# One level of Strassen's algorithm in the gate and up blocks of a gated network, with the way down in three parts

## The chip, the core and the metric

The kernel runs on one core of one Trainium2 chip. The metric is device time in microseconds (us) of one execution. Before the change it is 920.8 us, the median of three runs (919.7 to 921.03). One more execution was recorded by the hardware profiler; it took 920.15 us, and its trace spans 918.4 us from the first to the last instruction. All rows below come from that one execution.

## The reference

One layer of a streaming encoder on 512 tokens of width 1024, all in float32: a mixer (sliding-window attention beside gated linear attention), cross attention on 256 memory tokens, and a gated network with 2816 hidden units, each added to the residual, then a last normalisation. The change concerns the gated network and what stands at its two ends:

```python
def _rms(t, w):
    y = t * lax.rsqrt(jnp.mean(t * t, axis=-1, keepdims=True) + EPS)
    return y * w

def _swiglu(h, w_gate, w_up, w_down):
    return (jax.nn.silu(h @ w_gate) * (h @ w_up)) @ w_down

x = x + _swiglu(_rms(x, norm_ffn_w), w_ffn_gate, w_ffn_up, w_ffn_down)   # 1024 -> 2816 -> 1024
return _rms(x, norm_final_w)
```

## The kernel before, in words

Activations lie transposed: eight tiles of 128 features by 512 tokens are the residual (`res`). A float32 product is made of three products in a rounded format (`F32R`): each operand is split into a rounded high part and the rest (`split`, lines 93 to 100: a ScalarE copy, then a VectorE subtraction), and high x high, high x low and low x high are added up in PSUM. A block of 128 outputs by 512 tokens with a contraction over 1024 is thus 8 x 3 = 24 matmuls of 512 columns (`block`).

Weights come in units of 128 x 1024 float32 (512 KB). `unit` takes three tiles from the pool `wp`, loads R by SyncE's DMA queue, and splits it into H and L. Each of the tags R, H, L has three slots; a slot is free when the last instruction that uses its tile is done. PSUM has four banks with the tag `mm`, two `s`, one `t`, one `o`.

The program is traced in order, and a planner then makes a fixed order for each engine: of the instructions that are ready in its own reckoning it takes the one that stands earliest in the program, and it gives a tile any slot of its tag that is free. Where `manual_schedule` names an engine, that engine keeps the order of the program.

The stages around the change. The end of the cross attention adds to `res` (line 996) and splits `res` times the norm's weight (`weighted`, lines 97 and 98) into `zh` and `zl`. Then the gate and up blocks (lines 1007 to 1022): for each of 22 groups j of 128 hidden units, 24 matmuls for the gate and 24 for the up block, on tokens not yet divided by their root mean square. That factor comes from the norm `n2`, whose squares (ScalarE, line 195) and sums (VectorE, line 201) are written behind the blocks of j = 0; `finish` sums over partitions on TensorE, makes the root on VectorE, spreads it by TensorE, and ScalarE copies it to `n2.b` (line 224, tile `rb_n`). With `n2.b` VectorE scales the gate (line 1018), ScalarE applies Silu, VectorE multiplies by the up block (line 1020) and again by `n2.b` (line 1021), and the result is split into `ah[j]`, `al[j]`.

Last the way down: for each of eight blocks of 128 outputs, 66 matmuls over all 22 groups, the sum into `res` (line 1036), and the square for the last norm `n3`. The last block goes in two halves of 256 tokens, each with its own end of the norm, its own scaling (lines 1048 to 1054) and output DMAs.

Of the kernel before, what the change touches and what calls it, by code (L numbers as in the profile page):

```python
# [20 lines left out]
P = 128  # L21
S = 512
# [5 lines left out]
NF = DFF // P  # L28
EPS = 1e-6
NEG = -1.0e30  # L30
TGW = 328
DENSE = (10, 5, 11, 3, 1)


def build(tc, a, out):
# [56 lines left out]
    def split(hi, lo, src, scale=None):  # L92
# [3 lines left out]
        else:  # L96
# [2 lines left out]
                out=lo, in0=src, scalar=scale, in1=f(hi), op0=ALU.mult, op1=ALU.subtract  # L99
            )  # L100

    def unit_tiles():
        return [
            wp.tile([P, 1024], dt, tag=tag, bufs=3, name=uniq(tag)) for tag, dt in (("R", F32), ("H", F32R), ("L", F32R))
        ]

    def unit(src):
# [893 lines left out]
    mep_ctx.__exit__(None, None, None)  # L1001


    fp_ctx = pool("fp")
    fp = fp_ctx.__enter__()
    ah = [fp.tile([P, S], F32R, name=f"ah{j}") for j in range(NF)]
    al_ = [fp.tile([P, S], F32R, name=f"al{j}") for j in range(NF)]
    for j in range(NF):
        pg = ps_mm()
        block(pg, [(unit(a["w_fg"][j]), KC)], zh, zl)  # L1010
        pu = ps_mm()
        block(pu, [(unit(a["w_fu"][j]), KC)], zh, zl)
        if j == 0:
            for i in range(KC):
                n2.add(res[i])
            n2.finish()
        t = t2k()
        nc.vector.tensor_tensor(out=t, in0=pg, in1=n2.b, op=ALU.mult)  # L1018
        table_act(t, t, AF.Silu)
        nc.vector.tensor_tensor(out=t, in0=t, in1=pu, op=ALU.mult)  # L1020
        nc.vector.tensor_tensor(out=t, in0=t, in1=n2.b, op=ALU.mult)
        split(ah[j], al_[j], t)

    n3 = Norm("n3", S)
    for j in range(KC):
        units = []
        for k0 in range(0, NF, KC):
            nk_ = min(KC, NF - k0)
            units.append((unit(a["w_fd"][j][:, k0 * P : (k0 + nk_) * P]), nk_))

        W = S if j < KC - 1 else S // 2
        for c0 in range(0, S, W):
            cs = slice(c0, c0 + W)
            pb = ps_mm()
            block(pb[:, :W], units, [x[:, cs] for x in ah], [x[:, cs] for x in al_])
            nc.vector.tensor_tensor(out=res[j][:, cs], in0=res[j][:, cs], in1=pb[:, :W], op=ALU.add)
            n3.add(res[j][:, cs], cols=cs, last=j == KC - 1)
            if j < KC - 1:
                nc.scalar.activation(res[j], res[j], AF.Copy, scale=wo_w[:, j : j + 1])
                continue  # L1040
            n3.finish(cols=cs)
            for i in (7, 6, 0, 1, 2, 3, 4, 5):
                if i % 2 == (1 if i > 5 else 0):
                    fin = xwp.tile([P, S], F32R, tag="xw", bufs=16, name=uniq("fin"))
                    f3 = f(fin).rearrange("p (e c) -> p e c", e=2)
                o = f3[:, i % 2]
                if i == j:
                    nc.vector.scalar_tensor_tensor(
                        out=o, in0=res[i][:, cs], scalar=wo_w[:, i : i + 1], in1=n3.ps, op0=ALU.mult, op1=ALU.mult
                    )  # L1050
                elif i in (3, 5):
                    nc.gpsimd.tensor_tensor(out=o, in0=res[i][:, cs], in1=n3.b, op=ALU.mult)
                else:
                    nc.vector.tensor_tensor(out=o, in0=res[i][:, cs], in1=n3.ps, op=ALU.mult)
                if i % 2 == (0 if i > 5 else 1):
                    nc.sync.dma_start(out[i // 2][:, :, cs], f3)
    fp_ctx.__exit__(None, None, None)
    ctx.close()

# [70 lines left out]
```

## Time and profile before

| | |
|---|---|
| median of three runs | 920.8 us (919.7 to 921.03) |
| profiled execution | 920.15 us |
| its span | 918.4 us |
| TensorE matmul busy | 902.0 us (98%), 4318 matmuls |
| TensorE weight load busy | 746.2 us (81%) |
| VectorE busy | 557.3 us (61%) |
| ScalarE busy | 426.5 us (46%) |
| mean granted TensorE clock | 0.996 |
| HBM | 83.27 MB read, 93 GB/s over the span |

Matmuls are pipelined: one reports 0.39 us while the next starts 0.23 us after it. So the pace of TensorE is read from the distance of two starts, not from the duration of one, and the same holds for VectorE, where an instruction reports up to 0.09 us more than the distance to the next.

### The profile page before, as it was taken

What the parts mean: (1) busy time and instruction counts of PE and PEld (TensorE: products, weight loads), DVE (VectorE), ACT (ScalarE), POOL (GpSimd) and SP (SyncE); (2) the same over time, 40 slices, a digit from 0 to 9 for tenths busy, and PEclk for the clock granted to TensorE, in tenths of its full rate; (3) what the DMA queues carried; (4) which work ended last, traced back from release to release, by engine and by line L of the source; (5) the groups of instructions that cost most, each with busy time, mean ns of one, the idle gap of its engine ahead of it and who ended that gap; (6) DMA issues with size and microseconds to landing.
All of it is one profiled execution on the core that took longest, in us unless ns stands there. A gap on an engine that the chain in (4) does not pass through costs nothing.

```text
span 918.4 us, 11423 instructions
## 1 busy us (share of the span) xinstructions
PE 902.0 (98%) x4318; PEld 746.2 (81%) x4318; DVE 557.3 (61%) x1104; ACT 426.5 (46%) x760; POOL 7.0 (1%) x29
## 2 busy tenths in 40 slices
PE   9999999999999999999999999999999999999995
PEld 7898888887888787778888778888888888888885
DVE  6777888787343959966676996444444444323323
ACT  7576674556333838463345864222332233222220
POOL 1000000000000000000000000000000000000001
PEclk9999999999999999999999999999999999999998
DMA  7232222222222031425332223233222332333312
GB/s 249 92 115 70 69 70 69 70 69 69 92 94 91 23 115 46 144 87 155 120 115 92 70 77 107 92 97 110 92 92 92 99 107 86 99 91 103 87 41 92
DMA packets 29415, 86.11 MB, mean 94 GB/s; under 512 B 4048, under 2 KB 7760, under 8 KB 29360
## 3 DMA queue, kind: packets, MB, share of 16 engines
q1 hardware_dynamic: 29216, 85.37, 29.3%
q8 instruction: 34, 0.56, 0.3%
q14 instruction: 21, 0.17, 0.1%
q10 hardware_dynamic: 144, 0.00, 0.0%
HBM read 83.27 MB, written 2.10 MB: 93 GB/s over the span
## 4 chain that ended last, share of the span: by engine, by line
PE 89%; DVE 6%; ACT 3%; DMA 1%; issue 1%; SPq 0%; DVEq 0%; ACTq 0%
PE mm L76 80%; PE s L76 3%; PE o L76 3%; PE t L76 1%; DMA x<-in_xT 1%; DVE L L95 1%; PE t L540 1%; ACT pm L90 1%; PE mm L540 1%; DVE sl L95 1%; DVE on L743 1%; ACT H L94 0%; PE t L754 0%; DVE st L701 0%; DVE on L722 0%
## 5 line engine op out<-in xcount | busy, mean ns | idle before, releaser
L94 ACT CAST H<-R 128x1024 fp32r<-128x1024 f32 (+2 forms) x155 | 156.8, 1013 | 326.1 <-PE mm L76 251.4
L95 DVE TENSOR_TENSOR L<-R,H 128x1024 fp32r<-128x1024 f32 (+2 forms) x155 | 181.7, 1174 | 93.5 <-ACT H L94 93.1
L76 PE MATMUL mm<-xh,L 128*128 128x512 f32 x592 | 232.4, 393 | 0.0
L76 PE MATMUL mm<-xl,H 128*128 128x512 f32 x592 | 232.2, 392 | 0.0
L76 PE MATMUL mm<-xh,H 128*128 128x512 f32 x592 | 230.8, 390 | 0.0
L76 PEld LDWEIGHTS mm<-xh,H 128*128 128x128 f32 x592 | 111.2, 188 | 22.7
L76 PEld LDWEIGHTS mm<-xl,H 128*128 128x128 f32 x592 | 111.2, 188 | 22.3
L76 PEld LDWEIGHTS mm<-xh,L 128*128 128x128 f32 x592 | 111.2, 188 | 21.6
L76 PE MATMUL mm<-ah,H 128*128 128x512 f32 (+1 forms) x198 | 72.5, 366 | 0.0
L76 PE MATMUL mm<-ah,L 128*128 128x512 f32 (+1 forms) x198 | 72.4, 366 | 0.0
L76 PE MATMUL mm<-al,H 128*128 128x512 f32 (+1 forms) x198 | 72.3, 365 | 0.0
L76 PE MATMUL mm<-H,xh 128*128 128x512 f32 (+1 forms) x192 | 70.4, 367 | 0.0
L76 PE MATMUL mm<-L,xh 128*128 128x512 f32 (+1 forms) x192 | 70.3, 366 | 0.0
L76 PE MATMUL mm<-H,xl 128*128 128x512 f32 (+1 forms) x192 | 70.1, 365 | 0.0
L1020 DVE TENSOR_TENSOR t2k<-t2k,mm 128x512 f32<-128x512 f32 x22 | 15.0, 688 | 68.3 <-PE mm L76 67.6
L90 ACT ACTIVATE p<-sm,nm,sc 128x256 f32<-128x256 f32 (+1 forms) x64 | 36.3, 569 | 25.3 <-DVE es L514 20.4
L1018 DVE TENSOR_TENSOR t2k<-mm,rb_n 128x512 f32<-128x512 f32 x22 | 15.1, 691 | 44.9 <-PE mm L76 43.0
L76 PEld LDWEIGHTS mm<-ah,H 128*128 128x128 f32 x198 | 37.3, 189 | 6.1
L76 PEld LDWEIGHTS mm<-ah,L 128*128 128x128 f32 x198 | 37.3, 189 | 6.1
L76 PEld LDWEIGHTS mm<-al,H 128*128 128x128 f32 x198 | 37.3, 189 | 5.9
L76 PEld LDWEIGHTS mm<-H,xh 128*128 128x128 f32 x192 | 36.4, 190 | 5.2 <-issue 0.2
L76 PEld LDWEIGHTS mm<-L,xh 128*128 128x128 f32 x192 | 36.1, 188 | 5.3 <-DVE L L95 0.4
(299 smaller groups left out, 1365.2 us busy)
## 6 DMA issues: line engine op xcount, KB each, us to landing
R<-in_w_fg SPq DMA_DIRECT2D x22, 512.0 KB, 3.3
R<-in_w_fu SPq DMA_DIRECT2D x22, 512.0 KB, 3.3
R<-in_w_gate SPq DMA_DIRECT2D x16, 512.0 KB, 3.4
R<-in_w_fd SPq DMA_DIRECT2D x16, 512.0 KB, 3.5
x<-in_xT SPq DMA_DIRECT2D x16, 256.0 KB, 3.3
R<-in_w_q SPq DMA_DIRECT2D x8, 512.0 KB, 3.6
R<-in_w_attn_o SPq DMA_DIRECT2D x8, 512.0 KB, 3.3
R<-in_w_vg SPq DMA_DIRECT2D x8, 512.0 KB, 3.3
```

The costliest lines, as they stand in the source:

```text
L76: nc.tensor.matmul(o, lhsT=lhsT, rhs=rhs, start=start, stop=stop)
L90: last_table[0] = nc.scalar.activation(*args, **kw)
L94: nc.scalar.copy(out=hi, in_=src)
L95: nc.vector.tensor_tensor(out=lo, in0=src, in1=f(hi), op=ALU.subtract)
L540: nc.tensor.transpose(out=pt[:, i * P : (i + 1) * P], in_=prs[i // 2][:, i % 2, b * P : (b + 1) * P], identity=ident)
L743: nc.vector.scalar_tensor_tensor(out=on[t][:, vs], in0=on[t][:, vs], scalar=r[:, h : h + 1], in1=glaw, op0=ALU.mult, op1=ALU.mult)
L1018: nc.vector.tensor_tensor(out=t, in0=pg, in1=n2.b, op=ALU.mult)
L1020: nc.vector.tensor_tensor(out=t, in0=t, in1=pu, op=ALU.mult)
```

## The change

The gate and up blocks of groups 2 to 21 are made by one level of Strassen's algorithm (in Winograd's form): the two weight matrices of a group, each in two halves of the contraction, are one 2 x 2 of blocks, and the tokens, in two halves of 512 features and two halves of 256 tokens, the other. Seven products take the place of eight. Each product is 4 x 3 = 12 matmuls of 256 columns, so a group has 84 of them in place of 48 of 512. Groups 0 and 1 (`NPLAIN = 2`) stay as they were.

The token operands are sums of normalised tokens, so they need `n2.b`: `token_side` makes them once, behind the end of `n2` and ahead of the gating of group 0. `weight_side` makes the weight operands of each group: two loads, four pairs of H and L. `group` has three steps, each ended by a `yield`: products r11 and r21; then t2, t1, t3; then t4, r22 and the gating. TensorE keeps the written order: for groups 2 to 7 the first step of group j+1 stands ahead of the last step of group j; from group 8 a block of the way down stands between the second and the last step. The way down is in parts of 8, 8 and 6 groups: the first two are added to `res` between the groups, the third takes the place of the loop at the end. The pool `fw` takes the place of `wp` with three slots for R, four for H, four for L, and two of tag S for sums.

```diff
+NPLAIN = 2
-    wp = ctx.enter_context(pool("wp"))
+    wp_ctx = pool("wp", side="right")
+    wp = wp_ctx.__enter__()
...
+    wp_ctx.__exit__(None, None, None)
     fp = fp_ctx.__enter__()
+    fw_ctx = pool("fw", side="right")
+    units_from[:] = fw, (3, 4, 4)
+    PARTS = ((0, 8), (8, 16), (16, NF))
+    t0, t1 = slice(0, HS), slice(HS, S)
...
+    def token_side():
+        zn = []
+        for i in range(4):
+            t = f(fp.tile([P, 2, S], F32R, tag="a", bufs=8, name=uniq("zn")))
+            for e in range(2):
+                nc.vector.scalar_tensor_tensor(
+                    out=t[:, e], in0=res[2 * i + e], scalar=wf_w[:, 2 * i + e : 2 * i + e + 1], in1=n2.b,
+                    op0=ALU.mult, op1=ALU.mult,
+                )
+            zn.append(t)
+        def part(o, i, src):
+            hi, lo = (zc[o][:, 2 * i : 2 * i + 2, x, :] for x in range(2))
+            nc.scalar.copy(out=hi, in_=src)
+            nc.vector.tensor_tensor(out=lo, in0=src, in1=f(hi), op=ALU.subtract)
+        for i in range(2):
+            part("r11", i, zn[i][:, :, t0])
+        for i in range(2):
+            part("r21", i, zn[2 + i][:, :, t0])
...
+    def weight_side(j):
+        r0, r1 = (fw.tile([P, 1024], F32, tag="R", bufs=3, name=uniq("R")) for _ in range(2))
+        nc.sync.dma_start(r0, a["w_fgu"][j, :, 0:1024])
+        nc.sync.dma_start(r1, a["w_fgu"][j, :, 1024:2048])
+        q0, q1 = slice(0, 512), slice(512, 1024)
+        h0, l0 = pair_of(r0)
+        h1, l1 = pair_of(r1[:, q0])
+        sa = fw.tile([P, 2, 512], F32, tag="S", bufs=2, name=uniq("SA"))
+        nc.vector.tensor_tensor(
+            out=sa, in0=r1[:, None, q1].broadcast_to([P, 2, 512]), in1=r0.rearrange("p (e c) -> p e c", e=2), op=ALU.add
+        )
+        sb = fw.tile([P, 2, 512], F32, tag="S", bufs=2, name=uniq("SB"))
+        nc.vector.tensor_tensor(out=sb[:, 0], in0=sa[:, 0], in1=r0[:, q1], op=ALU.add)
+        nc.vector.tensor_tensor(out=sb[:, 1], in0=sb[:, 0], in1=r1[:, q0], op=ALU.add)
+        ha, la = pair_of(sa.rearrange("p e c -> p (e c)"))
+        hb, lb = pair_of(sb.rearrange("p e c -> p (e c)"))
+        return {
+            "r11": (h0[:, q1], l0[:, q1]), "r21": (h1[:, q0], l1[:, q0]), "t2": (hb[:, q0], lb[:, q0]),
+            "t1": (ha[:, q0], la[:, q0]), "t3": (ha[:, q1], la[:, q1]), "t4": (h0[:, q0], l0[:, q0]),
+            "r22": (hb[:, q1], lb[:, q1]),
+        }
+    def group(j):
+        w = weight_side(j)
+        pa, pb = ps_mm()[:, :HS], ps_mm()[:, :HS]
+        g = t2k()
+        product(pa, w, "r11", True, True)
+        nc.scalar.copy(out=g[:, t0], in_=pa)
+        product(pb, w, "r21", True, True)
+        nc.vector.tensor_tensor(out=g[:, t0], in0=pb, in1=g[:, t0], op=ALU.add)
+        yield
+        pc = ps_s()[:, :HS]
+        product(pa, w, "t2", False, True)
+        nc.scalar.copy(out=g[:, t1], in_=pa)
+        product(pc, w, "t1", True, True)
+        product(pa, w, "t3", False, True)
+        nc.scalar.copy(out=s3, in_=pa)
+        nc.vector.tensor_tensor(out=s3, in0=pc, in1=s3, op=ALU.subtract)
+        yield
+        product(pa, w, "t4", False, True)
+        product(pc, w, "r22", False, True)
+        nc.vector.tensor_tensor(out=g[:, t1], in0=g[:, t1], in1=pc, op=ALU.subtract)
+        table_act(g, g, AF.Silu)
+        nc.vector.scalar_tensor_tensor(out=g[:, t0], in0=pa, scalar=-1.0, in1=g[:, t0], op0=ALU.mult, op1=ALU.mult)
+        nc.vector.tensor_tensor(out=g[:, t1], in0=s3, in1=g[:, t1], op=ALU.mult)
+        hidden(j, g)
+        yield
...
-    for j in range(NF):
+    for j in range(NPLAIN):
         pg = ps_mm()
         block(pg, [(unit(a["w_fg"][j]), KC)], zh, zl)
         pu = ps_mm()
...
             n2.finish()
+            token_side()
...
+    with tc.manual_schedule(engines={mybir.EngineType.PE}):
+        at = {j: group(j) for j in range(NPLAIN, NF)}
+        next(at[NPLAIN])
+        for j in range(NPLAIN, NF):
+            next(at[j])
+            if j < PARTS[1][0]:
+                next(at[j + 1])
+            elif j < PARTS[2][0]:
+                down(0, j - PARTS[1][0])
+            else:
+                down(1, j - PARTS[2][0])
+            next(at[j])
+            if PARTS[1][0] <= j < NF - 1:
+                next(at[j + 1])
+        for i in range(NF - PARTS[2][0], KC):
+            down(1, i)
...
     for j in range(KC):
-        units = []
-        for k0 in range(0, NF, KC):
-            nk_ = min(KC, NF - k0)
-            units.append((unit(a["w_fd"][j][:, k0 * P : (k0 + nk_) * P]), nk_))
+        units = down_units(2, j)
```

The part of `token_side` that is left out makes, in the same way, the sums x1 to x4 (two VectorE instructions each, from tiles of tag S) and from them and `zn` the operands t2, t1, t3, t4 and r22: seven operands in all, two `part` calls each.

## Rows read from the trace of the kernel before

**Rows 1.** Engines over the whole span: busy us, share, instructions.
```profile
PE 902.0 (98%) x4318; PEld 746.2 (81%) x4318; DVE 557.3 (61%) x1104; ACT 426.5 (46%) x760; POOL 7.0 (1%) x29
```
**Rows 2.** Chain that ended last: start, us, what; its longest piece.
```profile
564.27 332.97 PE mm L76 x1500
```
**Rows 3.** Stages: length, busy (instructions) by engine, clock, DMA share, GB/s.
```profile
553.40:566.80 13.40, 13.07 (x65) 10.59 (x64) 7.18 (x17) 6.29 (x9) 0.00 (x0) 1.00 0.31 103
566.80:784.40 217.60, 217.60 (x961) 180.18 (x961) 102.39 (x123) 66.29 (x83) 0.00 (x0) 1.00 0.30 96
```
**Rows 4.** TensorE in order of time (start, us), last half block: 36 matmuls apart.
```profile
902.26 0.28 PE L76 MATMUL mm<-ah,L 128*128 128x256 f32 x1
...
906.57 0.28 PE L76 MATMUL mm<-ah,L 128*128 128x256 f32 x1
```
**Rows 5.** TensorE in order of time: the first matmul of group 2.
```profile
566.84 0.39 PE L76 MATMUL mm<-xh,H 128*128 128x512 f32 x1
```
**Rows 6.** VectorE and ScalarE in order of time, around the end of `n2`.
```profile
537.97 0.74 DVE L98 SCALAR_TENSOR_TENSOR xl<-x,wf_w,xh 128x512 fp32r<-128x512 f32 x1
538.63 0.68 DVE L996 TENSOR_TENSOR x<-x,mm 128x512 f32<-128x512 f32 x1
...
546.73 0.68 DVE L201 TENSOR_TENSOR acc_n<-acc_n,sq 128x512 f32<-128x512 f32 x1
...
556.94 0.69 DVE L201 TENSOR_TENSOR acc_n<-acc_n,sq 128x512 f32<-128x512 f32 x1 [0.70 <-ACT sq L195]
558.34 0.69 DVE L201 TENSOR_TENSOR acc_n<-acc_n,sq 128x512 f32<-128x512 f32 x1 [0.70 <-ACT sq L195]
...
561.11 1.23 DVE L95 TENSOR_TENSOR L<-R,H 128x1024 fp32r<-128x1024 f32 x1
562.25 0.15 DVE L171 SCALAR_TENSOR_TENSOR nwy<-nwt,nwy 128x4 f32<-128x4 f32 x1
...
564.31 0.59 ACT L224 COPY rb_n<-t 128x512 f32<-128x512 f32 x1 [4.49 <-PE t L76]
564.93 1.29 DVE L1018 TENSOR_TENSOR t2k<-mm,rb_n 128x512 f32<-128x512 f32 x2 [1.93 <-ACT rb_n L224]
...
568.08 1.28 DVE L1021 TENSOR_TENSOR t2k<-t2k,rb_n 128x512 f32<-128x512 f32 x2
569.28 1.22 DVE L95 TENSOR_TENSOR L<-R,H 128x1024 fp32r<-128x1024 f32 x1
570.42 1.28 DVE L95 TENSOR_TENSOR al<-t2k,ah 128x512 fp32r<-128x512 f32 x2
```
**Rows 7.** Groups of instructions: count, busy us, mean ns; the weight split and 256 columns.
```profile
L94 ACT CAST H<-R 128x1024 fp32r<-128x1024 f32 x59 | 62.2, 1054 | 188.8 <-PE mm L76 123.3 <-issue 65.6
L224 ACT COPY rb_n<-t 128x256 f32<-128x256 f32 x2 | 0.7, 372 | 7.2 <-PE t L76 7.2
```
**Rows 8.** All engines in order of time: the ends of the two halves.
```profile
897.28 0.42 DVE L1036 TENSOR_TENSOR x<-x,mm 128x256 f32<-128x256 f32 x1 [5.71 <-PE mm L76]
...
902.55 1.74 DVE L1054 TENSOR_TENSOR fin<-x,t 128x256 f32<-128x256 f32 x5
...
906.89 0.42 DVE L1036 TENSOR_TENSOR x<-x,mm 128x256 f32<-128x256 f32 x1 [2.61 <-PE mm L76]
...
912.20 1.74 DVE L1054 TENSOR_TENSOR fin<-x,t 128x256 f32<-128x256 f32 x5
```
**Rows 9.** Stages at the end, columns as in group 3.
```profile
905.00:907.00 2.00, 1.97 (x18) 1.88 (x16) 0.11 (x1) 0.00 (x0) 0.00 (x0) 1.00 1.03 344
...
912.00:914.00 2.00, 0.00 (x0) 0.00 (x0) 1.93 (x6) 0.00 (x0) 1.26 (x2) 0.50 0.07 25
```
**Rows 10.** TensorE's first matmuls, in order of time.
```profile
1.22 3.59 PE L76 MATMUL s<-t2k 128*128 128x512 bf16 x8 [1.22 <-DVE t2k L142]
4.66 0.79 PE L76 MATMUL o<-xh,h 128*128 128x512 f32 x1
...
6.47 0.37 PE L76 MATMUL mm<-H,xh 128*128 128x328 f32 x1
```

More of the change, by code (lines that the diff above doesn't have):

```diff
@@ new lines, in pair_of @@
+    def pair_of(src):
+        h = fw.tile([P, 1024], F32R, tag="H", bufs=4, name=uniq("H"))
+        lo = fw.tile([P, 1024], F32R, tag="L", bufs=4, name=uniq("L"))
+        n = src.shape[-1]
+        split(h[:, :n], lo[:, :n], src)
+        return h, lo
+    def weight_side(j):
[8 more added lines that the diff above has]
+            out=sa, in0=r1[:, None, q1].broadcast_to([P, 2, 512]), in1=r0.rearrange("p (e c) -> p e c", e=2), op=ALU.add
+        )
+        sb = fw.tile([P, 2, 512], F32, tag="S", bufs=2, name=uniq("SB"))
[8 more added lines that the diff above has]
+        }
@@ new lines, in product @@
+    def product(o, w, op, first, last):
+        h, lo = w[op]
+        x = zc[op]
+        for k in range(4):
+            ks = slice(k * P, (k + 1) * P)
+            for i, (l_, r_) in enumerate(prod3(h[:, ks], lo[:, ks], x[:, k, 0, :], x[:, k, 1, :])):
+                nc.tensor.matmul(
+                    o, lhsT=l_, rhs=r_, start=first and k == 0 and i == 0, stop=last and k == 3 and i == 2,
+                    skip_group_check=not first,
+                )
+    def group(j):
[8 more added lines that the diff above has]
+        pc = ps_s()[:, :HS]
+        s3 = tp.tile([P, S], F32, tag="sq", bufs=1, name=uniq("s3"))[:, t0]
+        product(pa, w, "t2", False, True)
[13 more added lines that the diff above has]
+        yield
@@ L1009, in build, with down_units, down_block, down @@
+    def down_units(p, i):
+        lo, hi = PARTS[p]
+        return [(unit(a["w_fd"][i][:, lo * P : hi * P]), hi - lo)]
+    def down_block(o, p, units, cs):
+        ks = range(*PARTS[p])
+        block(o, units, [act[k][0][:, cs] for k in ks], [act[k][1][:, cs] for k in ks])
+    def down(p, i):
+        pd = ps_mm()
+        down_block(pd, p, down_units(p, i), slice(0, S))
+        nc.vector.tensor_tensor(out=res[i], in0=res[i], in1=pd, op=ALU.add)
+    for j in range(NPLAIN):
         pg = ps_mm()
@@ L1034, in build @@
             pb = ps_mm()
-            block(pb[:, :W], units, [x[:, cs] for x in ah], [x[:, cs] for x in al_])
+            down_block(pb[:, :W], 2, units, cs)
             nc.vector.tensor_tensor(out=res[j][:, cs], in0=res[j][:, cs], in1=pb[:, :W], op=ALU.add)
@@ L1113 @@
         ),
[L1114 to L1115 removed]
+        "w_fg": w_fg[:NPLAIN],
+        "w_fu": w_fu[:NPLAIN],
+        "w_fgu": np.concatenate([w_fu[:, :, 512:], w_fg, w_fu[:, :, :512]], 2),
         "w_fd": _stationary(x["w_ffn_down"][0]),
```

53 lines of the change are left out of this document (47 added, 6 removed).

## The prediction

> **What bounds the kernel now.** I read four views. The engine line of the page comes first: TensorE reports 98% busy and VectorE 61% [rows 1]. Then the chain that ended last: from 564 us to the way down it is one unbroken piece of matmuls, 333 us long [rows 2]. So in this stage the time is the number of matmuls by their distance. Third, the stages: in 217.6 us of the gate and up blocks (20 groups) VectorE is busy for 102.4 us and ScalarE for 66.3 [rows 3], so both have room, but VectorE has only half of the time left. Last, the order of time around the place where the new work starts, at the end of the norm `n2`, because that work hangs on `n2.b`.
>
> **What the products save.** Twenty groups before: 960 matmuls of 512 columns in 217.6 us, 0.2267 us each [rows 3]. After: 20 x 84 = 1680 of 256 columns. The last block of the way down has that shape, with a weight load for each matmul as the products have: 36 of them from 902.26 to 906.57, 0.1197 us each [rows 4]. 1680 x 0.1197 = 201.1 us, so 16.5 us go. Half the columns cost 53% of the time, which is why it is not an eighth of 217.6. The way down has as many matmuls as before, but the first 16 groups of its last block are now 48 of 512 columns in place of 96 of 256: 96 x 0.1197 - 48 x 0.2267 = 0.6 us less. Together **-17.1 us**.
>
> A rule speaks for more. The Trainium skill (TensorE: Matmul & The Clock Gate, section Back-to-back issue gap) has N/2.4 + 2.5 ns between matmuls at full clock, 109.2 ns for 256 columns and 215.8 for 512; by it the products would take 183.5 in place of 207.2 us, 23.7 less. The rows are some 11 ns above it at both sizes, and that is lost 1680 times in place of 960; the trace decides.
>
> **What the token side costs at the start.** Before, `n2.b` is ready at 564.90 (ScalarE's copy starts at 564.31 and takes 0.59) [rows 6], and group 2's matmuls follow group 1's at 566.84 without a break [rows 5]. Now nothing is left for TensorE after group 1 but products whose operands come behind `n2.b`, and they all go over VectorE. Distances of two starts there: 0.60 us for 128x512 (two from 568.08 to 569.28), 1.14 for 128x1024 (569.28 to 570.42), 0.66 for the form with a scalar (537.97 to 538.63), and 0.35 for 128x256 (1.74 / 5) [rows 6, 8]. The token side is 8 scalings (5.3 us), 6 sums at 0.60 and 2 at 0.66 (4.9), 12 low parts at 0.60 and 2 at 0.66 (8.5): 18.7 us.
>
> What is queued behind it matters more. Group 2 needs two `mm` banks, and the plain groups 0 and 1 hold all four until VectorE has read them, which needs `n2.b` too and stands behind `token_side` in the program. The planner takes the earliest instruction that is ready: at 564.93 the scaling of groups 0 and 1 went in one after the other because the next step of group 0 waited for ScalarE, and at 561.11 a weight split went in between two steps of the norm's chain [rows 6]. The token side is nearly always ready (ScalarE's 14 high parts, at most 0.6 us each, run beside the scalings), so I put the freeing of the banks at its end: 564.9 + 18.7 + 0.7 = 584.3. TensorE stands still from 566.8: **+17.5 us**. If the banks come free early, the sum of VectorE's work gives nearly the same: before group 3's second step can run, it has the 18.7, eight gating instructions (4.8), the last low part of group 2 (1.1), two evictions (0.7) and group 3's weights (four of 1024 and three of 512: 6.4), 31.7 us, up to 596.6; TensorE without a stop would be there after the seven products of group 2 and the first two of group 3, 9 x 12 x 0.1197 = 12.9 us, at 579.7. That is +16.9. The strided views (two rows of 256) are not in the trace: as two 256-wide instructions they would cost 0.70 for 0.60, 2 us more over some twenty; I take the contiguous price, the nearest.
>
> `n2` itself comes later. Its sums alternate with ScalarE's squares, 1.40 us a step where nothing interferes (556.94 to 558.34) [rows 6]; a weight split in a gap of VectorE delays it, and four of group 2 (low parts and sums) now lie there, where VectorE is busy for 7.2 of 13.4 us [rows 3]. One split more on the chain, **+1.1** (0 to 4; if the planner takes the squares earlier, less than nothing: the rival below).
>
> After such a stop the clock is low. At the end of the kernel the granted clock is 1.00 up to the last matmuls and 0.50 from 912 on, 5 us after the last dense matmul [rows 9]; half of 2.4 is 1.2 GHz. At the start, the matmuls from 1.22 to 6.47 us come at 0.45 to 0.79 us each for 512 columns [rows 10], at half pace or less: 5.2 us that do the work of half of it. So **+2.6** (0 where VectorE is still the later one, 5 if the clock takes longer). The Trainium skill (same page, section Part 1: The HAM clock gate) also has these two levels; here the trace shows the fall and no return from it in mid-kernel.
>
> **What the groups cost.** In groups 2 to 7 VectorE has 4 x 1.14 + 3 x 0.60 for the weights and 5 x 0.35 + 0.6 for the rest, 8.7 us, in 10.05 us of matmuls: 87%, so it does not set the pace by its sum. From group 8 a block of the way down (5.4 us) comes to it with 1.7 us of VectorE, which leaves more room.
>
> The slots do bind. A group needs four pairs H and L, and there are four. For groups 3 to 8 `hb` gets a slot when the previous group's t4 is done; r22 (12 x 0.12 = 1.44) and the two matmuls of t2 that need only the high part (0.24) are all that runs until its low part is due. It takes a ScalarE cast (1.05 [rows 7]) and a VectorE subtraction (1.23 to its end [rows 6]): 2.4 with the hand-overs. 0.7 us short, six times: **+4.2** (0 to 10, if other splits stand ahead of it on either engine). From group 8 on t4 and r22 lie ahead of the next first step (2.9 us), which covers it.
>
> The products that add to a bank again (t2, t3, t4 on `pa`, r22 on `pc`) wait for the copy that reads it: 0.37 us [rows 7], under the 1.44 of another product, and even behind a 1.05 us cast in ScalarE's queue (1.42) nearly hidden. I take 0; with a second cast ahead, 1.1 us in each of 20 groups. Loads: 1 MB in 10 us is 105 GB/s beside 96 before [rows 3]; nothing.
>
> **The end.** The last block's halves are now 18 matmuls each (2.2 us), so the second half's chain starts 2.2 us behind the first's, where before it was 906.89 - 897.28 = 9.6 [rows 8], and both need VectorE: from the sum at 906.89 to the last scaling at 913.94 is 7.05 us, and the small steps and scalings of the first half, some 4 us, now lie in it or just ahead of it. My estimate of what collides is half of the scalings (1.74 + 0.4), **+1.0** (0 to 2.5).
>
> **Sum:** -17.1 + 17.5 + 1.1 + 2.6 + 4.2 + 1.0 = +9.3 us on the profiled 920.15, that is 929.5; the median of the three runs is 0.65 higher, so 930.
>
> **Rivals.** (a) *The backlog on VectorE is smaller: faster.* `n2`'s sums take 11.6 us for six steps from 546.73 to 558.34 [rows 6]; at 1.40 they would take 8.4, and with the first one taken as soon as two residuals are there they would end some 4 us earlier still. With `n2.b` 7 us earlier, the stop shrinks to 10, the clock and the slots cost nothing: -17.1 + 10 + 1 = -6, about 915. Even with the slots and the end as above it decides where `n2.b` comes before 558: -17.1 + 10.6 + 5.2 + 1.3 for the clock is nothing. For it: the squares need only `res`. Against it: the splits of `zh`, `zl` and the units stand ahead in the program, and more of them now. (b) *The copies wait behind two casts*: 1.1 us in 20 groups, 22 on the whole, less 8 where the stop has been counted too high: about 944. For it: ScalarE has three 1024-wide casts in each group; against: with three copies of 0.37 and three 512-wide instructions of 0.59 [rows 6, 7] they take only 6 us of 10. (c) *Half the columns take half the time*, 0.1133 us: 1680 x 0.0064 = 10.7 us less, 919. Against it: the 36 matmuls of just this shape [rows 4]. By the spacing that the Trainium skill's page on TensorE gives (above) it would be 923.
>
> **How the numbers follow.** Forecast 0.58 (its own range 921 to 940), (a) 0.22, (b) 0.15, (c) 0.02, others 0.03. A measurement here tells 0.2% (1.8 us) from nothing. Faster: (a) but for a small part, and some of (c) and the others, 0.21; same: the low edge of the forecast and (a)'s upper one, 0.09; slower: 0.70. For 8 in 10 the range reaches from the lower part of (a) to (b): 912 to 944.
>
> **What would show it.** Right: TensorE idle for some 15 to 20 us from about 567 with VectorE near 100% busy up to about 600; a granted clock of 0.5 at the first products; idle of 0.5 to 1 us at t2 of groups 3 to 8, ended by the low part; 256-column matmuls at 0.12 us. Wrong: a first product before 575, a 256-column distance other than 0.12, or idle time at t2 and t3 in all groups, ended by ScalarE's copies.

## The result, and the profile after

The changed kernel takes 943.73 us (median of four runs, 943.36 to 944.29) against 920.36 for the kernel before: 1.0254 times the time, 95% interval 1.0237 to 1.0272. The forecast was 930; the sign was right, the loss two and a half times as large. The profiled execution took 944.29 us, its span 942.5, so 24.1 us more than before in the span.

The engine line of the page, which answers [rows 1]: TensorE is busy for less time than before, and VectorE for 107 us more.

```profile
PE 895.1 (95%) x4990; PEld 763.7 (81%) x4990; DVE 663.9 (70%) x1290; ACT 486.5 (52%) x874; POOL 6.9 (1%) x29
```

The chain that ended last (start, us, what) is no longer one piece of 333 us, as in [rows 2]. The token side stands in it, then a piece of products for each group, then pieces of 36 products and 24 matmuls of the way down in turn: 4.08 / 36 = 0.1133 us and 5.59 / 24 = 0.2329 us.

```profile
568.84 5.39 DVE zn L1048 x8
602.33 4.16 PE mm L1134 x35
663.07 3.94 DMA R<-in_w_fgu
675.30 5.59 PE mm L78 x24
683.62 4.08 PE mm L1134 x36
```

Stretches of the span, with the columns of [rows 3]: behind the plain groups (576.9) TensorE stands still, VectorE does not; the clock is at 0.50 where the products begin for the second time.

```profile
553.40:566.80 13.40, 13.35 (x60) 10.52 (x58) 7.87 (x18) 5.05 (x7) 0.00 (x0) 0.95 0.40 126
576.90:585.80 8.90, 0.14 (x1) 0.01 (x1) 8.90 (x16) 5.02 (x8) 0.00 (x0) 0.78 0.00 0
585.80:595.80 10.00, 4.44 (x25) 4.25 (x25) 10.00 (x16) 6.03 (x10) 0.00 (x0) 0.67 0.15 52
595.80:602.40 6.60, 5.87 (x26) 5.58 (x27) 5.07 (x6) 1.22 (x2) 0.00 (x0) 0.50 0.41 125
602.40:660.00 57.60, 49.39 (x418) 48.38 (x418) 43.70 (x63) 29.82 (x45) 0.00 (x0) 1.00 0.27 87
669.60:673.90 4.30, 4.30 (x24) 4.30 (x25) 3.93 (x7) 1.63 (x3) 0.00 (x0) 0.62 0.41 119
672.00:905.00 233.00, 233.00 (x1580) 213.00 (x1580) 153.45 (x216) 101.01 (x148) 0.00 (x0) 1.00 0.33 102
```

TensorE in order of time; in brackets the idle time ahead of a row and what ended it. Before, group 2 followed without a break at 566.84 [rows 5]. Now the first plain block waits for its weights' high part (548.88), the first product (585.82) for the bank that L1191 frees, t2 of group 2 (595.75) for the high part of the sum SB, and t2 of group 3 (611.27) for a low part.

```profile
545.06 0.39 PE L78 MATMUL mm<-omh,L 128*128 128x512 f32 x1
548.88 0.80 PE L78 MATMUL mm<-xh,H 128*128 128x512 f32 x1 [3.44 <-ACT H L96]
...
576.65 0.39 PE L78 MATMUL mm<-xh,L 128*128 128x512 f32 x1
585.82 0.76 PE L1134 MATMUL mm<-zc_r,H 128*128 128x256 f32 x2 [8.78 <-DVE t2k L1191]
...
595.75 0.80 PE L1134 MATMUL mm<-zc_t,H 128*128 128x256 f32 x2 [5.54 <-ACT H L96]
597.27 0.58 PE L1134 MATMUL mm<-zc_t,L 128*128 128x256 f32 x1 [0.73 <-DVE L L97]
611.27 0.39 PE L1134 MATMUL mm<-zc_t,L 128*128 128x256 f32 x1 [1.74 <-DVE L L97]
```

VectorE and ScalarE around the end of `n2`, answering [rows 6]. The copy to `n2.b` starts 3.9 us later than before. SA (587.39) and SB (592.13) follow only when x2 (read last at 585.59, for x4) and x4 (read last at 588.52) are done with their slots. At 608.86 the sum SA of the next group stands in VectorE's queue ahead of the low part of SB (610.00) for which t2 waits.

```profile
568.22 0.59 ACT L230 COPY rb_n<-t 128x512 f32<-128x512 f32 x1 [4.22 <-PE t L78]
584.99 0.68 DVE L1191 TENSOR_TENSOR t2k<-mm,rb_n 128x512 f32<-128x512 f32 x1
585.59 1.28 DVE L1082 SCALAR_TENSOR_TENSOR x<-x,zn 128x512 f32<-128x512 f32 x2
587.39 1.22 DVE L1112 TENSOR_TENSOR SA<-R,R 128x1024 f32<-128x1024 f32 x1
588.52 1.29 DVE L1057 TENSOR_TENSOR zc_t<-x,zc_t 128x512 fp32r<-128x512 f32 x2
592.13 0.68 DVE L1117 TENSOR_TENSOR SB<-SA,R 128x512 f32<-128x512 f32 x1
596.00 1.22 DVE L97 TENSOR_TENSOR L<-SB,H 128x1024 fp32r<-128x1024 f32 x1
...
607.60 1.23 DVE L97 TENSOR_TENSOR L<-SA,H 128x1024 fp32r<-128x1024 f32 x1
608.86 1.23 DVE L1112 TENSOR_TENSOR SA<-R,R 128x1024 f32<-128x1024 f32 x1
610.00 1.22 DVE L97 TENSOR_TENSOR L<-SB,H 128x1024 fp32r<-128x1024 f32 x1
```

The view of waits of TensorE from 600 to 905 us (us in total, times, longest) has a single line, these low parts:

```profile
PE mm L1134 <- DVE L L97: 10.2, 6, 1.9
```

The ends of the two halves [rows 8]: the second half's sum on TensorE (930.52) waits for the first half's last scaling to leave the bank `t`.

```profile
922.86 0.42 DVE L1223 TENSOR_TENSOR x<-x,mm 128x256 f32<-128x256 f32 x1
926.29 0.41 DVE L1223 TENSOR_TENSOR x<-x,mm 128x256 f32<-128x256 f32 x1
928.64 1.74 DVE L1241 TENSOR_TENSOR fin<-x,t 128x256 f32<-128x256 f32 x5
930.52 0.56 PE L78 MATMUL t<-ones,acc_n 128*128 128x2 f32 x2 [2.72 <-DVE fin L1241]
936.31 1.74 DVE L1241 TENSOR_TENSOR fin<-x,t 128x256 f32<-128x256 f32 x5
```

### The profile page after: what moved, and what is told of

It reads as the page before. It is cut to its first block, busy times and chain, and to the rows that moved or that the text cites. A ratio compares the mean times of both kernels' runs of the same rounds, so it can differ in the third digit from the quotient of the medians.

```text
span 942.5 us, 13120 instructions
## 1 busy us (share of the span) xinstructions
PE 895.1 (95%) x4990; PEld 763.7 (81%) x4990; DVE 663.9 (70%) x1290; ACT 486.5 (52%) x874; POOL 6.9 (1%) x29
## 4 chain that ended last, share of the span: by engine, by line
PE 83%; DVE 11%; ACT 3%; issue 2%; DMA 1%; SPq 0%; DVEq 0%; ACTq 0%
PE mm L78 56%; PE mm L1134 13%; PE s L1134 5%; PE o L78 3%; DVE L L97 3%; PE s L78 3%; PE t L78 1%; ACT H L96 1%; PE t L546 1%; ACT pm L92 1%; DVE zn L1048 1%; DVE xl L100 1%; PE mm L546 1%; DVE zc_t L1057 1%; DVE sl L97 1%
## 5 line engine op out<-in xcount | busy, mean ns | idle before, releaser
L96 ACT CAST H<-R 128x1024 fp32r<-128x1024 f32 (+4 forms) x155 | 147.8, 955 | 244.8 <-PE mm L78 135.5
L97 DVE TENSOR_TENSOR L<-R,H 128x1024 fp32r<-128x1024 f32 (+4 forms) x155 | 170.9, 1104 | 49.9 <-ACT H L96 49.5
L78 PE MATMUL mm<-xh,H 128*128 128x512 f32 x272 | 108.5, 399 | 3.4 <-ACT H L96 3.4
L78 PE MATMUL mm<-a,H 128*128 128x512 f32 (+1 forms) x364 | 111.4, 388 | 0.0
L78 PE MATMUL mm<-xh,L 128*128 128x512 f32 x272 | 109.6, 403 | 0.8 <-DVE L L97 0.8
L78 PE MATMUL mm<-xl,H 128*128 128x512 f32 x272 | 109.5, 403 | 0.0
L1134 PE MATMUL mm<-zc_t,H 128*128 128x256 f32 x480 | 87.0, 280 | 5.5 <-ACT H L96 5.5
L1134 PEld LDWEIGHTS mm<-zc_t,H 128*128 128x128 f32 x480 | 74.9, 191 | 7.0 <-ACT H L96 5.7
L1134 PE MATMUL mm<-zc_t,L 128*128 128x256 f32 x240 | 68.0, 283 | 10.9 <-DVE L L97 10.9
L78 PE MATMUL mm<-a,L 128*128 128x512 f32 (+1 forms) x182 | 70.6, 388 | 0.0
L78 PEld LDWEIGHTS mm<-xh,L 128*128 128x128 f32 x272 | 51.6, 190 | 11.8 <-DVE L L97 1.5
```

Of the source, the lines that this page charges most:

```text
L78: nc.tensor.matmul(o, lhsT=lhsT, rhs=rhs, start=start, stop=stop)
L96: nc.scalar.copy(out=hi, in_=src)
L97: nc.vector.tensor_tensor(out=lo, in0=src, in1=f(hi), op=ALU.subtract)
L1134: nc.tensor.matmul(o, lhsT=l_, rhs=r_, start=first and k == 0 and i == 0, stop=last and k == 3 and i == 2, skip_group_check=not first,)
```

## The experiments

In the order in which they ran. Ratios are to the kernel before, with their 95% intervals.

**The place of the weight pool (e1, e2).** On the kernel before. e1 moves the weight pool to the right side; e2 also closes it and opens another for the gated network's weights.

```diff
-    wp = ctx.enter_context(pool("wp"))
+    wp_ctx = pool("wp", side="right")
+    wp = wp_ctx.__enter__()
```

> The kernel before with one edit: the pool of the weight units is opened on the right side of SBUF, as in the change; it stays open to the end. Theory (placement): the distance of two matmuls depends on where their operands lie; the changed kernel lost 2.8 us of its 24.1 before the gated network begins, so this kernel is 2 to 4 us slower than before by the last matmul of the cross attention (542.2 us becomes 544 to 546), and more matmuls of 512 columns stand 0.231 to 0.236 us apart in place of 0.227. Rival: those 2.8 us come from the planner's order, which the gated network's edit upset; then this kernel takes the time of before, within 1 us.

> The kernel before with the pool on the right as in e1_wp_right, and in addition closed ahead of the gated network, where a new pool of the same three slots of R, H and L takes its place; no Strassen. Theory (pool switch): the first unit of the gated network can't be split until the old pool's last tiles are free, so TensorE waits some 5 us at the start of group 0 and comes back at the low clock: 5 to 8 us slower than e1_wp_right. Rival: the changed kernel's late start came from VectorE and ScalarE being busy with the residual's splits, whatever the pool; then it takes the time of e1_wp_right.

e1: 932.92 us, 1.0138 (1.0123 to 1.0153): 12.6 more, by moving one pool alone. e2: 939.99, 1.0210 (1.0195 to 1.0226), 7.1 more than e1, with the first plain matmul 3.8 us behind the one ahead of it and the clock down behind it, as in the changed kernel at 548.88. The second was foreseen; of the first the direction was, with 2 to 4 us in place of 12.6. The longest piece of e1's chain, 332.97 us before [rows 2]:

```profile
567.95 342.09 PE mm L77 x1500
```

**The sums' slots, and the order of the steps (e3, e4).** On the changed kernel. e3 gives x1 to x4 slots of the activations instead of the two that SA and SB use; e4 puts t4 and r22 of group j ahead of the first step of group j+1 in groups 2 to 7 too.

```diff
-            return fw.tile([P, 4, HS], F32, tag="S", bufs=2, name=uniq(name))
+            t = f(fp.tile([P, 2, S], F32R, tag="a", bufs=8, name=uniq(name)))
+            return t.rearrange("p e (c h) -> p (e c) h", h=HS)
```

```diff
             if j < PARTS[1][0]:
-                next(at[j + 1])
+                pass
...
             next(at[j])
-            if PARTS[1][0] <= j < NF - 1:
+            if j < NF - 1:
                 next(at[j + 1])
```

> The changed kernel with one edit: the four sums x1 to x4 of the token side take slots of the tag a (free at that time) in place of the two slots of the tag S, which they shared with the weight sums SA and SB. Theory (shared slots): in the changed kernel group 2's weight sums and two of its low parts, 5.3 us of VectorE, came behind the token side because x1 to x4 had the slots; now they come ahead of the end of the norm n2, and TensorE's second stop (590.05 to 597.27 us, ahead of product t2) shrinks by 4 to 7 us; the whole is 4 to 7 us faster than the changed kernel, at 937 to 940. Rival: VectorE's sum of work binds there whatever the slots (it has no gap from 569 to 600 us); then less than 1 us.

> The changed kernel with one edit: for groups 2 to 7 TensorE takes the last step of group j ahead of the first step of group j+1 (as for the later groups), in place of behind it. Theory (slots and order): groups 3 to 8 lose 2.07 us each at product t2, since hb gets its slot only after t4 of the group before and a weight sum of the next group stands ahead of its low part on VectorE; with the first step between, that loss goes, and what comes is some 0.5 us a group for t4 behind the copy of its bank: 11.6 us a group becomes 10 to 10.3, the whole 8 to 10 us faster, 934 to 936. Rival: VectorE's load (9.5 us busy in each 11.6) binds; then the period stays above 11 us.

e3: 938.39, 5.3 less; the wait at t2 of group 2 is gone, and the first product comes at 589.09, 3.3 us later, with all that t2 needs there. e4: 937.31, 6.4 less; the period of the groups falls from 11.59 to 10.68 us, less than I had put. What is left (1.14 us a group) now lies ahead of t4, which follows t3 on the same bank and waits for ScalarE's copy out of it:

```profile
605.64 0.50 PE L1134 MATMUL mm<-zc_t,H 128*128 128x256 f32 x2 [0.91 <-ACT s L1155]
```

**The last bank (e5).**

```diff
-            pb = ps_t()
+            pb = ps_o() if cols else ps_t()
```

> The changed kernel with the row of reciprocal roots in the two half-width ends of the last norm spread into the bank of tag o in place of the single bank of tag t; nothing else. In the changed kernel TensorE ends its last matmul 16.6 us before the span's end (before: 11.5), and the second half's sum over partitions waits 2.72 us for VectorE's scaling of the first half, which reads that one bank. Theory (one bank is the cause): the second half's sum starts as soon as its squares are there, 4 to 5 us go, 939 to 940. Rival (VectorE's scalings of the first half are in the way, whatever the bank): less than 1.5 us, above 942.

942.6 us (940.47 to 945.62): too wide to tell 1.1 us from nothing. In its trace the second half's sum no longer waits, yet from the last dense matmul to the end are 14.7 us, against 16.6 in the changed kernel and 11.8 before: VectorE's scalings of the first half now stand ahead of the second half's root. So by the trace the bank is some 2 us and VectorE's order the rest; by the times of the runs even these 2 us are not shown.

**Side or address (e6, e7, e8).** By the programs' memory plans, which no row here prints, weights and moving operands of the gated network have the same address modulo 128 bytes before (32 and 32), and on the right side they differ (96 and 32). e6 leaves the pool on the left and puts 64 bytes behind it; e7 is e1 with 64 bytes to the right of the pool; e8 is the changed kernel with 64 bytes ahead of the products' token operands.

```diff
     wp = ctx.enter_context(pool("wp"))
+    padl = ctx.enter_context(pool("padl"))
+    padl.tile([P, 16], F32, name="padl")
```

```diff
+    padr = ctx.enter_context(pool("padr", side="right"))
+    padr.tile([P, 16], F32, name="padr")
     wp_ctx = pool("wp", side="right")
```

```diff
+    fp.tile([P, 16], F32, name="pad0")
     zc = {o: fp.tile([P, 4, 2, HS], F32R, name=f"zc_{o}") for o in OPS}
```

> The kernel before with the weight pool where it was, on the left, and 64 bytes put between it and the pools behind it, so that the operands that move through TensorE start 64 bytes further on; nothing else. Before, the weights and the moving operands of the gated network have the same address modulo 128 (both 32); now they differ by 64. Theory (TensorE's distance depends on whether the two operands have the same address modulo 128): 512-column matmuls of the gated network 0.2335 us apart in place of 0.2267, that is 9 us on the 1364 between 570 and 890 us, 1 to 4 us in the stages before, 930 to 934 in all; the 256-column ones of the last block 0.1138 in place of 0.1198, 0.6 us back. Rival (what costs is that the pool lies on the right, far from its operands): 920, as before.

> The kernel before with the weight pool on the right (932.92 us by itself), and 64 bytes put to the right of it, so that the weights have the same address modulo 128 as the moving operands; nothing else. Theory (same or different address modulo 128): 512-column distance back to 0.2267, and 430 matmuls of the stages before that differed in the kernel before now agree as well, 6.7 ns each or 2.9 us at most: 917 to 921. Rival (the right side is what costs): 932 to 934.

> The changed kernel with 64 bytes put ahead of the products' token operands and of the activations behind them, so that they have the same address modulo 128 as the weights (both 96); nothing else. Theory: the 256-column products come 0.1198 us apart in place of 0.1135, as in the last block of the kernel before: 1680 x 0.0062 = 10.4 us more, less where they wait anyway (some 1 us of a group's stall is then covered in groups 3 to 8, 4 us); 318 matmuls of 512 columns of the way down 0.2267 in place of 0.2335, 2.1 us less: 947 to 953. Rival (the products' distance is a matter of their shape or of their weights' order): 0.1135 stays, 941 to 944.

e7: 919.18, 0.9991 (0.9982 to 1.0000). The whole loss of e1 is in 64 bytes. e6: 924.91, 1.0055 (1.0040 to 1.0070), two fifths of e1's loss: here the moving operand is the one at 96, and the distance is 0.2289 us in place of e1's 0.2333. So the address counts, and which operand is shifted counts too, which I had not expected. The same chain piece in e7 and then in e6 (332.97 before, 342.09 in e1):

```profile
562.06 332.98 PE mm L79 x1500
```
```profile
565.89 336.02 PE mm L78 x1500
```

e8: 949.58, 5.9 more than the changed kernel; the pieces of 36 products go from 4.08 to 4.32 us, 0.1200 each, the distance of [rows 4].

```profile
683.39 4.32 PE mm L1135 x36
```

**Taking the losses away together (e9 to e12).** e9 is the changed kernel with e3, e4 and e5, and with the weight pool kept open on the right (R, H and L three slots each), ha and la in single slots of their own.

```diff
-    wp_ctx.__exit__(None, None, None)
...
-        ha, la = pair_of(sa.rearrange("p e c -> p (e c)"))
+        ha = fw.tile([P, 1024], F32R, tag="HA", bufs=1, name=uniq("H"))
+        la = fw.tile([P, 1024], F32R, tag="LA", bufs=1, name=uniq("L"))
+        split(ha, la, sa.rearrange("p e c -> p (e c)"))
```

e10 adds addresses (`zc` in a pool of its own behind 64 bytes, 192 bytes fewer ahead of all), e11 a third plain group, e12 halves for the last two blocks of the way down.

```diff
-NPLAIN = 2
+NPLAIN = 3
...
-        pg = ps_mm()
+        pg = ps_mm() if j < 2 else ps_s()
```

> The changed kernel with four edits: the sums of token_side in slots of the activations (alone 5.3 us less), t4 and r22 of group j ahead of r11 and r21 of group j+1 for the groups 2 to 7 as well (alone 6.4 less), the last norm's row in the bank of tag o (alone 1 to 2 less), and new here: the weight pool is not closed and opened again at the gated network but kept, still on the right, with its three slots for R, H and L; only ha, la and the sums have slots in a pool of their own. Theory: the first gate block no longer waits for the pool (7.1 us, as the same switch cost the kernel before), but the first product waits for VectorE's work behind n2.b, so the stop behind the plain groups grows by what n2.b does not come earlier: n2.b some 4 us earlier, stop 3 us longer, 926 to 929. Rival: the four simply add up, 943.7 - 5.3 - 6.4 - 1.5 - 7.1 = 923.4. Second rival: one slot each for ha and la and three for the rest stall the groups again, above 930.

> e9 with addresses chosen by what the 64-byte runs showed: the moving operands of all 512-column matmuls at the same address modulo 128 as the weights (192 bytes saved ahead of them by sharing small tiles), the products' token operands 64 bytes off, as they are now. Theory: 512-column distance 0.2267 instead of 0.2335 in the stages before (2.8 us, plus up to 2.9 for those that differed in the kernel before), in the plain groups (0.6, which the stop may give back) and in the way down (510 x 0.0067 = 3.4); products stay at 0.1135: 5 to 9 us less than e9. Rival (only the kernel before gains from it; here other waits set the time): less than 2 us.

> e10 with three plain groups in place of two, the third one's gate and up blocks in the two banks of tag s, so that TensorE has 10.9 us of work while VectorE makes the products' token operands and frees the banks. Theory (the stop behind the plain groups is for want of work that needs no n2.b): the stop of 9 to 14 us goes all but a rest below 3, and with it the half clock at the first products; a plain group costs 10.9 - 9.5 = 1.4 more than one of products: 9 to 13 us less than e10. Rival (VectorE's backlog only moves the stop behind the third group): 4 us less at most.

> e11 with the last two blocks of the way down in halves of 256 tokens, first half of both, then second half of both, so that 36 matmuls (4.3 us) lie between the ends of the two halves in place of 18 (2.2). Theory (the second half's chain runs into VectorE's scalings of the first because only 2.2 us lie between them): from the last dense matmul to the end 14.7 or so becomes 12 to 13, 2 to 3 us less than e11. Rival: the end does not depend on it, within 1 us.

e9: 939.09 (933.55 to 940.32), 1.0194; its second rival was nearest. The plain groups now end at 570.29, 6.4 us earlier, and the first product comes no earlier. Rows of e9 on ScalarE, VectorE and TensorE:

```profile
569.79 0.59 ACT L229 COPY rb_n<-t 128x512 f32<-128x512 f32 x1 [5.80 <-PE t L77]
570.41 5.39 DVE L1045 SCALAR_TENSOR_TENSOR zn<-x,wf_w,rb_n 128x512 f32<-128x512 f32 x8 [2.68 <-ACT rb_n L229]
588.97 1.28 DVE L1191 TENSOR_TENSOR t2k<-mm,rb_n 128x512 f32<-128x512 f32 x2
589.80 0.77 PE L1134 MATMUL mm<-zc_r,H 128*128 128x256 f32 x2 [19.12 <-DVE t2k L1191]
```

That is the stop of the prediction, undisguised: 589.80 - 569.79 = 20.0 us from the copy to the first product, and 0.59 + 18.7 + 0.7 = 20.0 were foreseen. The other trace times of copy and first product: e3 569.08 and 589.09, e10 565.35 and 585.35, e11 566.00 and 586.03, e16 565.38 and 585.39, all 20.0. In the changed kernel and e4 it is 17.6, because the planner let one L1191 in before the end of the token side. So what the pool's closing costs the plain groups is not paid twice: it fills a stop that is there anyway. e9 pays elsewhere: 1.57 us ahead of each t4 where e4 had 1.14, and products 0.1178 us apart from group 8 on (13 groups x 84 x 4.4 ns = 4.8 us). e10: 932.86, 6.2 less than e9, as forecast, though its products did not stay at 0.1134: at full clock they are 0.1178 us apart in all groups, and so in e11 and e12. e11: 926.71, 6.2 less than e10, between its two theories: the stop is 10 us in place of 19.5, for the banks still come free at the token side's end, and the 586.03 stays. e12: 926.17, no difference: from the last dense matmul to the end it is 1.6 us shorter, but the dense work ends 1.3 us later, and 0.95 of that stands ahead of the first product already.

**The start in another order (e13 to e18).** e13 is the changed kernel with `n2.add` behind each residual, both plain groups' blocks ahead of any gating, and `token_side` between the two gatings. e14 is e13 with e3, e4, e5 and the addresses of e10; e15 has three plain groups besides; e16 is e14 with the start as the change has it.

```diff
             zl.append(lo)
+            n2.add(res[j])
+    n2.finish()
...
-            for i in range(KC):
-                n2.add(res[i])
-            n2.finish()
-            token_side()
...
+    for j, (pg, pu) in enumerate(plain):
+        if j == 1:
+            token_side()
```

> The changed kernel with another order at the start of the gated network: the squares and sums of n2 stand right behind each residual, the blocks of both plain groups ahead of the gating, and token_side between the gating of group 0 and that of group 1. Nothing is added or taken away. Theory (n2.b and the banks behind token_side set the first product): n2.b at 553 to 558 in place of 568.8, the first product at 577 to 580 in place of 585.8 (TensorE's plain blocks then end just ahead of it), t2 some 5 us earlier as well, 8 to 13 us less: 931 to 936. Rival (the sum of VectorE's work sets it, in whatever order): the weights' splits now come later by what the norm comes earlier, less than 4 us, above 940.

> e13, with the sums of token_side in slots of the activations, t4 and r22 ahead of the next r11 and r21 throughout, the last norm's row in the bank of tag o, and the addresses of e10 (512-column matmuls at the same address modulo 128, the products' tokens where they were). Theory: the parts add, 5 for the sums (less what e13 has already taken), 6.4 for the order, 1 to 2 for the bank, 6 for the addresses: 912 to 919. Rival (they overlap at the start, where all of them end at VectorE): 920 to 926. If the products run at 0.1178 in place of 0.1135, 7 us more.

> e14 with three plain groups. Theory (e14 still has a stop of some us behind group 1, which 10.9 us of plain work covers, for 1.4 us): 2 to 8 less than e14. Rival (e14 has no stop left): 1 to 2 more.

> e14 with the start of the changed kernel (without e13's order). Theory (the losses found one by one add up): 943.7 - 5.3 - 6.4 - 1.5 - 6 = 924.5, 921 to 928, which is within the prediction's own range; with products at 0.1178, 931. Rival (they overlap): above 932 with products at 0.1135.

e13: 945.29, 1.5 more. The norm comes 3.7 us earlier (copy at 564.57) and buys nothing: VectorE's fixed order has the token side behind three steps of group 0's gating, which wait for TensorE's blocks, and SA waits for the sums' slots as before. Its VectorE and TensorE:

```profile
571.68 0.69 DVE L1196 TENSOR_TENSOR t2k<-t2k,rb_n 128x512 f32<-128x512 f32 x1
572.28 0.75 DVE L1050 SCALAR_TENSOR_TENSOR zn<-x,wf_w,rb_n 128x512 f32<-128x512 f32 x1
...
593.33 1.24 DVE L1114 TENSOR_TENSOR SA<-R,R 128x1024 f32<-128x1024 f32 x1
```
```profile
598.75 0.80 PE L1136 MATMUL mm<-zc_t,H 128*128 128x256 f32 x2 [14.46 <-ACT H L96]
```

e14: 929.37; e15: 927.02; e16: 926.99, so with the other losses away too the new start gains nothing. In e14 the first product comes at 576.29, 9.1 us ahead of e16's, and then t2 waits for ScalarE's copy and for a low part:

```profile
586.02 0.79 PE L1139 MATMUL mm<-zc_t,H 128*128 128x256 f32 x2 [6.74 <-ACT t2k L1150]
590.38 0.58 PE L1139 MATMUL mm<-zc_t,L 128*128 128x256 f32 x1 [3.56 <-DVE L L97]
```

e16 is 16.7 us under the changed kernel, by taking away the slots, the order, the bank and the addresses. One by one these were 5.3 + 6.4 + 1.1 and about 7 for the addresses (an estimate: 3.3 in the way down, 2.8 ahead of the gated network, 0.6 in the plain groups): some 20. The parts add up to within 2 us, if one allows for its products, 36 of which take 4.08 us up to group 7 and 4.24 from group 8 on, as in e9, which is 4.8 us on the other side.

```profile
608.66 4.08 PE mm L1137 x36
666.47 4.24 PE mm L1137 x36
```

e17 (from e16) and e18 (from e11) have three plain groups and another order at the start; e18 also has the token operands back at the address of the changed kernel modulo 512.

```diff
+    first_weights = weight_side(NPLAIN)
+    for j, (pg, pu) in enumerate(plain):
...
         hidden(j, t)
+        if j == 0:
+            token_side()
```

> e16 with three plain groups (the third in the banks of tag s) and with the start written in another order: the blocks of all three, the squares and sums of n2 behind the first, then the first product group's weights, then the gating of group 0, token_side, the gating of groups 1 and 2. Theory (the stop of 12.2 us in e16 is for want of work that needs no n2.b, and of banks): plain blocks end at about 584, the first product follows within 2 us, t2 waits less than 3: one group of products less behind a first product at the same time as in e16, so 9 to 13 us less, 914 to 918, just under the kernel before. Rival (VectorE's backlog moves the stop into the first groups of products): 921 to 926.

> e11 (pool kept, three plain groups) with the same order at the start, and the token operands at the address of the changed kernel modulo 512. Theory: first product at 578 to 582 in place of 586, t2 within 3 us: 5 to 9 us less than e11's 926.7, 917 to 922; if the address decides the products' distance (0.1135 in place of 0.1178), 7 us less again, 910 to 915. Rival (ha and la wait for slots and VectorE waits with them): no gain, 925 to 929.

922.24, 1.0025 (1.0015 to 1.0036), and 922.47, 1.0028 (1.0017 to 1.0039): the best, and still some 2 us slower than the kernel before. e17 lies in the range of its rival, e18 just above that of its theory. In e17 the first product follows the plain groups without a stop, in e18 a stop of 3.4 us comes behind its first matmul; a stop at t2 has taken its place (6.4 in e17, 7.3 in e18), and it is ScalarE that ends it. Rows of e17: the copy that frees the bank stands in ScalarE's queue behind four casts of the token side, which wait for VectorE.

```profile
588.21 1.82 ACT L1058 CAST zc_t<-x 128x512 fp32r<-128x512 f32 x3 [0.84 <-DVE x L1080]
591.82 0.62 ACT L1058 CAST zc_t<-x 128x512 fp32r<-128x512 f32 x1 [1.79 <-DVE x L1085]
592.34 0.37 ACT L1148 COPY t2k<-mm 128x256 f32<-128x256 f32 x1
592.76 0.80 PE L1137 MATMUL mm<-zc_t,H 128*128 128x256 f32 x2 [6.41 <-ACT t2k L1148]
```

## Why the prediction was wrong, step by step

Each term, set as a time of TensorE from the first product on, as the prediction had it and as the trace of the changed kernel has it (us):

| | predicted | measured |
|---|---|---|
| first product (584.3 + 1.1) | 585.4 | 585.8 |
| products by their distance (1680 x 0.1197; x 0.1140) | 201.1 | 191.5 |
| way down (510 of 512 columns, 36 of 256) | 119.9 | 124.2 |
| wait at t2 of group 2 | 0 | 6.7 |
| waits at t2 of groups 3 to 8 | 4.2 | 11.1 |
| lost at half clock | 2.6 | 6.5 |
| last dense matmul to the end (11.8 before + 1.0) | 12.8 | 16.6 |
| sum (of unrounded terms) | 926.0 | 942.5 |

The first column adds up to 926.0 and not to 918.4 + 9.3 = 927.7: the rest is 1.7 us of small hand-overs of the kernel before that the terms leave where they were.

The stop ahead of the first product came as foreseen. What failed is what the sum had behind it: the wait at t2 of group 2 and the slower way down stood at nothing, and the waits at t2 of the later groups, the half clock and the end were put too low. These steps add 25.6 us to the forecast, and the products, closer together than foreseen, take 9.6 back.

- **What the token side costs: right in mechanism, and in size partly by luck.** The first product comes 0.4 us from the forecast, by the bank behind the token side, and 20.0 us behind the copy in five other traces. In the changed kernel two misses cancel: the copy comes 3.9 us later and not 1.1 (2.8 of them lie ahead of the gated network already), and the product follows it after 17.6 us and not 20.0. And the plain groups end at 576.9 and not at 566.8, so the trace shows a stop of 8.9 and not of 17.5. The step "the pool `fw` takes the place of `wp`" had no price at all; e1, e2 and e9 show it, and that the stop swallows it.
- **Group 2's splits and sums ("four of group 2 (low parts and sums) now lie there", ahead of `n2`'s end): wrong for the sums.** They came behind nearly all of the token side: SA and SB share two slots with x1 to x4, and the prediction gave the tag S no term. 6.7 us; e3 has no such wait and is 5.3 us faster.
- **"The slots do bind", mis-sized:** 1.85 us a group, six times, where 0.7 stood. The late slot for hb was right; what was missed is that SA of the next group goes ahead of lb's subtraction in VectorE's order (608.86). e4 takes 0.9 us a group away with the order of the steps alone.
- **1680 x 0.1197: wrong by 9.6 us, to the other side.** The distance of rival (c), at a chance of 0.02, was nearest: most products are 0.1133 us apart, some 0.1178, 0.1140 on the mean. The row of [rows 4] had the shape and not the addresses; e8, with 64 bytes, brings its 0.1200 back. The weight pool's address costs the way down 3.3 us (510 x 0.0065) of the 4.3 in the table; the rest lies in its last block. The Trainium skill (TensorE: Matmul & The Clock Gate, section Back-to-back issue gap) gives N / 2.4 + 2.5 ns for a matmul by itself, which is 109.2 and 215.8 ns at these widths; the runs show two or more distances for each, all above it.
- **The clock: right in kind, mis-sized.** The products met half clock three times and not once: from 585.82 to 588.6 behind a stop of 8.8 us, from 595.75 to 602.4 behind one of 5.5, and for most of 669.6 to 673.9 (0.62 on the mean) behind one of 1.9 with a load in its chain (663.07). The five stops of 1.6 to 1.7 us at t2 of groups 3 to 7 left the clock at 1.00 (602.4 to 660). 6.5 us in all, where 2.6 stood.
- **The end: mis-sized.** The prediction counted collisions on VectorE and missed the single bank `t`; the trace of e5 gives about 2 us to the bank, which its times are too wide to show.
- **Rival (a)** asked for an `n2.b` before 558. e13 and e14 had the copy 3.7 and 5.5 us earlier than the same kernel with the old start, at 564.57 and 559.90, and were not faster. But they changed the order of the gating as well, and neither came before 558, so (a) itself is not tested. **Rival (b)**, copies behind casts, gave nearly the measured time, 944, for a reason that the changed kernel does not show: its waits at t2 and t3 are ended by ScalarE's copies nowhere. Such waits come in e14, e17 and e18 at t2 of the first group of products, and in e4, e9 and e16 at t4, once the other waits are gone.

What stays open: why the products of e9, e16 and e18 run 0.1134 us apart up to group 7 and 0.1178 from group 8 on (in the changed kernel it is 0.1133 there); that e18's operands have the changed kernel's address modulo 512 did not bring it back. It is not the place in the program alone: in the changed kernel three of the seven products between two stops run at 0.1178 in groups 3 to 7 and the other four at 0.1134, and in e17 whole groups alternate up to group 7. The same products, on the same token operands, run at the one distance in some groups and at the other in others, so the address of the token operands does not decide between these two; whether the weights' slots, the banks or the stops do is not shown. And with some 2 us between e17 and the kernel before, whether a still better order of VectorE and ScalarE in the first 30 us would make the change pay was not tried.

## What to carry to other kernels

A saving on a bound engine is paid in work for the others, and the place where all of it comes due at once (here the end of a norm) sets the price: follow each engine's queue from there, slot by slot and bank by bank, past the first product to the second and third. Price every line of a diff, a pool that merely moves too. A duration taken from a row holds for its operands' addresses as well as its shape; look for a second row of that shape at other addresses, and for a second stretch of the same kernel.

## What the runs showed of the hardware that I had not expected

The distance of matmuls of this rounded format changes when one operand moves by 64 bytes against the other. Sorted by their addresses modulo 128 bytes, as the memory plans give them (only shifts of 64 and 192 bytes were tried): 512 columns: 0.2267 us when they agree (kernel before, e7), 0.2333 when the moving operand is at 32 and the weights at 96 (e1), 0.2289 the other way round (e6). 256 columns: 0.1197 to 0.1200 when they agree (kernel before, e8), 0.1133 or 0.1178 when they differ (both in the changed kernel and in e16), so the narrow matmul wants what the wide one doesn't. What in the chip does this no run here shows. The Trainium skill (SBUF — State Buffer, section SBUF: two separate sides) says that PE, ACT and DVE's dedicated port pair "never wait on anyone"; e1 and e7, 13.7 us apart by 64 bytes with the same instructions, show that TensorE's pace is not free of where its operands lie; whether it waits at the memory is not shown.
